# Row factors turned in 32x32 squares and stored in runs of 128 bytes, convolution states packed for their store, last columns stored later

## The chip, the cores and the metric

One Trainium2 chip, of which the kernel uses one core. The time is the device time of one execution in microseconds (us); the runs are compared by their median. The core has TensorE (PE in the profile, with its weight loads as PEld), VectorE (DVE), ScalarE (ACT), GpSimd (POOL) and SyncE (SP). SP computes nothing here: it issues transfers. ACT and POOL issue transfers as well. All transfers share 16 DMA engines. Each engine works through its own instructions in order, and waits on semaphores where an instruction needs another engine's result or a transfer.

## The reference

One layer of a hybrid decoder over 4096 prompt tokens and 64 sample tokens (8 sequences of 8), width 1024, all in float32:

```python
h = _rmsnorm(x, g_pre)
z = h @ w_in
cb, cc, ch, cg, q, k, v, ag, mq, mg = _split_cols(z)
u = cc * ch
up = jnp.concatenate([conv_buf, u], axis=1)
conv = conv_w[0] * up[:, 0:t] + conv_w[1] * up[:, 1:t + 1] + conv_w[2] * up[:, 2:t + 2]
out_a = jax.nn.silu(cg) * cb * conv
new_conv = up[:, -CONV_BUF:]
...
y = jnp.concatenate([out_a, out_b, out_c], axis=-1) @ w_out
return x + _rmsnorm(y, g_post), new_conv, new_k, new_v
```

`out_b` is sliding-window attention, `out_c` attention into 256 memory tokens. Two things matter here. `_rmsnorm` needs one factor per token, the reciprocal root of the mean square of its row. And `new_conv`, the last two columns of `u` of every sequence, is an output: `o_convs` for the 8 sample sequences, `o_convp` for the prompt.

## The kernel before

**Tiling.** The 4160 tokens (64 sample tokens first) form 8 blocks of 520, each of two halves of 260. Tokens lie along the free dimension and channels on the 128 partitions. The projection `w_in` is done in three phases, each over a part of its columns and over all 8 blocks. In phase 0 the first two blocks are plain products (`plain_block`, eight steps each); every other block of every phase takes seven products of a Strassen-like scheme, one step each, of block sums such as `T1`, `T2`. A step multiplies one half block, split into a high and a low part (`hi`, `lo`), by the weight parts, three passes in all. The third phase also prepares the memory keys and the first attention blocks; after it come attention and the output projection `w_out`.

**Row factors.** The factor of a token is the same number for all channels, so a block needs a row of 520 factors that is spread over the 128 partitions. `row_step` squares and sums 104 tokens at a time (tokens on partitions, `nat`), five times for a block, so the 520 sums stand in a tile `r` of 104 partitions by 5 columns: token 104 i + p of the block is at partition p, column i. POOL turns the sums into factors (lines 315 and 316). The factors of block 2 go another way (`rows_diag` and `rows_product`), and block 0's are used that way too in phase 0. For the seven blocks other than 2, POOL stores the 520 factors to a row in DRAM, `rowd`, each value 4 bytes from a place of its own (line 321). `rows_load` (line 284) then lets SP load that row to all partitions (`rb`), and `scale` (line 363) multiplies the block's half blocks by it. `row_queue` runs once in each step of phase 0; it sends the loads of `nat` and counts `row_spreads` down, so that `rows_load` is issued in the fourth step from the one that stored the row. It is in SP's order, so if the row has not been written, SP waits there with all loads behind it: the weights `ws` for later phases (line 234), the next `nat`, and the next half blocks `x` and `place` (line 271).

**Convolution states.** In phase 1 `finish_conv` (from line 475) makes `u`. In block 0 POOL multiplies the sample tokens' part into `us` (line 485), 128 x 8 x 10 values with two old columns first, and the last two columns of each sequence are stored from there: 1024 pieces of 8 bytes for each of two channel tiles. In the last block the two last columns (`ub_prev`, tile `tail`) are stored, 128 pieces of 8 bytes for each of the two tiles.

**Order.** In phase 0 and from phase 2 on, each engine keeps the order in which the program is written; in phase 1 the framework orders the work. `store` sends from POOL in phase 0. Later it puts the store on `late`, and `flush` issues it from SP in the next step. A transfer also waits until the transfer eight before it of the same kind (eight semaphores for those of POOL, eight for those of SP and ACT) has landed, since it takes over its semaphore.

Of the kernel before, what the change touches and what calls it, by code (L numbers as in the profile page):

```python
# [8 lines left out]
F32 = mybir.dt.float32  # L9
# [6 lines left out]
P = 128  # L16
# [5 lines left out]
NB = 8  # L22
# [30 lines left out]
def hybrid_layer(ctx: ExitStack, tc: tile.TileContext, a: dict):  # L53
# [22 lines left out]
    V, TE, S, G = (InOrder(engine) for engine in (nc.vector, nc.tensor, nc.scalar, nc.gpsimd))  # L76

    const = ctx.enter_context(tc.tile_pool(name="const", bufs=1))
    tiny = ctx.enter_context(tc.tile_pool(name="tiny", bufs=3))
# [9 lines left out]
    G.memset(mhalf, -0.5)  # L89
    gmem = const.tile([P, KT], F32, name="gmem")  # L90
    convw = const.tile([P, 2, 3], F32, name="convw")

    zs = const.tile([P, 14, NS], F32, name="zs")

# [3 lines left out]
    rowd = [tc.dram_tile([2 * HW], F32, name=f"rowd{b}") for b in range(NBLK)]  # L98
# [99 lines left out]
    def store(dst, src):  # L198
        if store_queue[0] is G:
            G.dma_start(dst, src)  # L200
        else:
            late.append(lambda: DMA.dma_start(dst, src))

    def temp(name):
        return tp.tile([P, 2 * HW if 1 in zp else 2 + 2 * HW], F32, tag="t", name=name)
# [69 lines left out]
    RG = 104  # L275
# [4 lines left out]
    row_loads, row_spreads = [], {}  # L280

    def rows_load(b, again=False):
        rows[b] = (temp(f"rb{b}")[:, : 2 * HW] if again else natp.tile([P, 2 * HW], F32, tag="rb", name=f"rb{b}"))
        DMA.dma_start(rows[b], rowd[b].partition_broadcast(P))

    def row_load(j):
        if j < 5 * NBLK:
            g = RG * j - NS
            if 2 <= j < 10 or 12 <= j < 14:
                t = (wa if j < 7 or j == 12 else wb).tile([P, 2, 512], F32, tag="w", name=f"nat{j}")  # L290
                t = nat[j] = t.rearrange("p a n -> p (a n)")
            else:
                t = nat[j] = natp.tile([P, D], F32, tag="nat", name=f"nat{j}")
            if g < 0:
                DMA.dma_start(t[:NS], a["x_s"])
                DMA.dma_start(t[NS:RG], a["x_p"][: RG - NS, :])
            else:
                DMA.dma_start(t[:RG], a["x_p"][g : g + RG, :])

    def row_step():  # L300

        j = sq[0]
        if j == 5 * NBLK:
            return
        b, i = divmod(j, 5)
        if i == 0:
            nat["r"] = tiny.tile([P, 8], F32, tag="r", name=f"r{b}", bufs=3)
        r, t = nat["r"], nat.pop(j)
        S.activation(t[:RG], t[:RG], AF.Square, accum_out=r[:RG, i : i + 1])  # L309
        if j in (10, 11) or j >= 14:  # L310
            row_loads.append(after_nat[0])
            after_nat[0] += 1
        sq[0] += 1
        if i == 4:
            G.tensor_scalar(r[:RG, 0:5], r[:RG, 0:5], 1.0 / D, EPS, op0=ALU.mult, op1=ALU.add)
            G.tensor_tensor(r[:RG, 0:5], r[:RG, 0:5], mhalf[:RG, 0:5], op=ALU.pow)
            if b in (0, PLAIN_BLOCKS):
                nat["factors"] = r
            if b == PLAIN_BLOCKS:
                return  # L320
            G.dma_start(rowd[b].rearrange("(i p) -> p i", p=RG), r[:RG, 0:5])
            if b > 0:
                row_spreads[b] = 4

    def rows_diag():

# [14 lines left out]
    def row_queue():  # L341

        for j in row_loads:
            row_load(j)
        row_loads.clear()
        for b in [b for b, n in row_spreads.items() if n == 1]:
            rows_load(b)
        for b in list(row_spreads):
            row_spreads[b] -= 1
            if row_spreads[b] == 0:  # L350
                del row_spreads[b]
# [68 lines left out]
    def flat(z):  # L420
        return z.rearrange("p a n -> p (a n)")
# [37 lines left out]
            V.tensor_copy(zs[:, zsi, :], th[:, :NS])  # L459
        store(md[idx, :, tokens(b)], th)  # L460

    ub_prev, us_of = [None, None], []

    def us_load():
        for ct in range(2):
# [9 lines left out]
    def finish_conv(b, ct, zc, zh, zg, zb):  # L475
        zc, zh, zg, zb = (flat(z) for z in (zc, zh, zg, zb))
        n = 2 * HW
        ns = NS if b == 0 else 0
        m = n - ns
        V.scalar_tensor_tensor(zg, zb, 0.5, zg, op0=ALU.mult, op1=ALU.mult)  # L480
        ub = temp(f"ub{b}_{ct}")[:, : 2 + m]
        if ns:
            us = us_of[ct]
            V.memset(ub[:, 0:2], 0.0)
            G.tensor_tensor(us[:, :, 2:10], zc[:, :ns].rearrange("p (b t) -> p b t", b=NB),
                            zh[:, :ns].rearrange("p (b t) -> p b t", b=NB), op=ALU.mult)
            store(a["o_convs"][ct], us[:, :, 8:10])
        else:
            V.tensor_copy(ub[:, 0:2], ub_prev[ct])
        V.tensor_tensor(ub[:, 2:], zc[:, ns:], zh[:, ns:], op=ALU.mult)  # L490
        ub_prev[ct] = tiny.tile([P, 2], F32, tag=f"tail{ct}", name=f"tail{b}_{ct}", bufs=2)
        V.tensor_copy(ub_prev[ct], ub[:, m : m + 2])
        if b == NBLK - 1:
            store(a["o_convp"][ct], ub_prev[ct])
        acc = temp(f"cacc{b}_{ct}")[:, :n]
        if ns:

            dst, t = (x[:, :ns].rearrange("p (b t) -> p b t", b=NB) for x in (acc, zc))
            G.tensor_scalar(dst, us[:, :, 0:8], convw[:, ct, 0:1], None, op0=ALU.mult)
            for i in (1, 2):  # L500
                G.tensor_scalar(t, us[:, :, i : i + 8], convw[:, ct, i : i + 1], None, op0=ALU.mult)
                G.tensor_tensor(dst, dst, t, op=ALU.add)
        for i in range(3):
            if i == 0:
                V.tensor_scalar(acc[:, ns:], ub[:, 0:m], convw[:, ct, 0:1], None, op0=ALU.mult)
            else:
                V.scalar_tensor_tensor(acc[:, ns:], ub[:, i : i + m], convw[:, ct, i : i + 1], acc[:, ns:], op0=ALU.mult, op1=ALU.add)
        V.tensor_tensor(acc[:, ns:], acc[:, ns:], zg[:, ns:], op=ALU.mult)
        if ns:
            G.tensor_tensor(mix_s[:, ct, :], acc[:, :ns], zg[:, :ns], op=ALU.mult)  # L510
        store(md[ct, :, 2 * HW * b + ns : 2 * HW * b + n], acc[:, ns:])
# [65 lines left out]
    def next_block(ph, b, p):  # L577

        nph, nb = (ph, b + 1) if b + 1 < NBLK else (ph + 1, 0)
        load = lambda o: lambda: x_of(nph, nb, o)  # L580
        ready = lambda o: lambda: x_ready(nph, nb, o)
        jobs = []
        if nph < 2:
            jobs += {0: "B11", 3: "B21 B12", 4: "B22"} .get(p, "").split() if ph == 0 else \
                    {0: "B11", 3: "B21", 4: "B12", 5: "B22"}.get(p, "").split()
            jobs = [load(o) for o in jobs]
        if ph == 0:
            jobs.insert(0, row_queue)
            if 1 <= p < 4:
                jobs.append(row_step)  # L590
        if p == (0 if nb else 1) and nph == 1 and nb < PLAIN_BLOCKS:
            jobs.append(lambda: rows_load(nb, nb > 0))
        if nph < 2:
            jobs += [ready(o) for o in {4: "B11", 5: "B21" if nph else "B21 B12", 6: "B12 B22" if nph else "B22"}.get(p, "").split()]
        if ph == 0 and 4 <= p < 6:
            jobs.append(row_step)
        if nph < 2:
            if p == 6:
                jobs.append(lambda: t_sum(nph, nb, "T1"))
        return jobs  # L600
# [286 lines left out]
    def v_load(k):  # L887
        third["v", k] = t = temp(f"vl{k}")[:, :512]
        DMA.dma_start(t, vd[:, NS + 512 * k : NS + 512 * k + 512])
# [91 lines left out]
    last = NBLK - 1  # L981
# [11 lines left out]
    def input_projection():  # L993
        for i, (ph, b, p) in enumerate(steps):
# [22 lines left out]
            jobs = list(pending.pop(i, ()))  # L1017
# [4 lines left out]
                jobs += next_block(ph, b, p)  # L1022
            if (ph, b, p) == (0, last, 2):
                jobs.append(us_load)
            if ph == 1 and NP_ * b + p + 2 in V_TURNS:
                jobs.append(lambda k=V_TURNS.index(NP_ * b + p + 2): v_load(k))
            if ph == 1 and NP_ * b + p in V_TURNS:
# [28 lines left out]
            if (ph, b, p) in SWITCH:  # L1056
                jobs = SWITCH[ph, b, p]() + jobs
# [660 lines left out]

    blocks = [Block(b) for b in (*range(31), 32, 31)]
    input_projection()  # L1720
    open_attention()
    chunk_load(2)
# [166 lines left out]
```

## Time and profile before

| | |
|---|---|
| median of 3 runs | 1458.19 us (1456.69 to 1459.25) |
| the profiled execution's own time | 1455.13 us |
| its span, first to last instruction | 1453.4 us |
| ACT busy | 756.0 us (52%) |
| POOL busy | 447.1 us (31%) |
| DMA | 337.27 MB, mean 232 GB/s |
| granted TensorE clock, mean | 0.999 |

The profile is of one execution. A row of the waits reads: engine and tile and line that waited, what it waited for, us in total, times, longest. A row of the windows reads: stretch in us from the span's start, its length, then busy us and instructions of PE, PEld, DVE, ACT and POOL, the granted clock, the DMA engines' busy share, and GB/s. A row of the timeline reads: start, length, engine, line, operation, out<-in, shapes, and in brackets the idle time ahead of it and what ended it. Program names carry no buffer numbers there: `lo_3T` is a low part in block 3, `place` a half block with a place of its own. SPq and POOLq are the queues' own instructions.

### The profile page before, as it was taken

What the parts mean: (1) busy time and instruction counts of PE and PEld (TensorE: products, weight loads), DVE (VectorE), ACT (ScalarE), POOL (GpSimd) and SP (SyncE); (2) the same over time, 40 slices, a digit from 0 to 9 for tenths busy, and PEclk for the clock granted to TensorE, in tenths of its full rate; (3) what the DMA queues carried; (4) which work ended last, traced back from release to release, by engine and by line L of the source; (5) the groups of instructions that cost most, each with busy time, mean ns of one, the idle gap of its engine ahead of it and who ended that gap; (6) DMA issues with size and microseconds to landing.
All of it is one profiled execution on the core that took longest, in us unless ns stands there. A gap on an engine that the chain in (4) does not pass through costs nothing.

```text
span 1453.4 us, 30932 instructions
## 1 busy us (share of the span) xinstructions
PE 1442.0 (99%) x11453; PEld 1324.3 (91%) x11453; DVE 1206.5 (83%) x1899; ACT 756.0 (52%) x1868; POOL 447.1 (31%) x622
## 2 busy tenths in 40 slices
PE   9999999999999999999999999999999999999998
PEld 9999999999999999999999999978777787777777
DVE  6879888899998877799678778998998889888853
ACT  6776665566522222234445534656566555655641
POOL 0223323212300000000002224275665566556661
PEclk9999999999999999999999999999999999999999
DMA  9999999896866644475987978999988899998773
GB/s 266 160 275 232 293 269 277 238 307 215 226 223 198 192 136 150 140 273 143 323 276 228 290 231 266 324 261 238 238 217 224 215 258 228 238 237 223 233 220 105
DMA packets 212124, 337.27 MB, mean 232 GB/s; under 512 B 55301, under 2 KB 126213, under 8 KB 211941
## 3 DMA queue, kind: packets, MB, share of 16 engines
q1 hardware_dynamic: 159189, 226.29, 52.7%
q0 software_dynamic: 44144, 78.68, 21.3%
q10 hardware_dynamic: 8640, 30.33, 6.7%
q8 instruction: 91, 1.49, 0.5%
q14 instruction: 60, 0.49, 0.1%
HBM read 192.48 MB, written 110.15 MB: 208 GB/s over the span
## 4 chain that ended last, share of the span: by engine, by line
PE 82%; DMA 8%; DVE 4%; issue 3%; ACT 2%; SPq 1%; POOL 1%; POOLq 0%; ACTq 0%; DVEq 0%
PE c L397 46%; PE y L1675 24%; PE pv L1144 5%; PE ws L1144 3%; DMA place<-in_xt 2%; PE xs L1144 2%; DMA nat<-in_x_p 2%; DMA wr_3A<-in_w_in 1%; PE mem_acc L825 1%; DMA md<-th 1%; DVE z L649 1%; DMA x_1B<-in_xt 1%; DMA vd<-v 1%; DMA wr_3S<-sd6S 1%; DMA w<-s 0%
## 5 line engine op out<-in xcount | busy, mean ns | idle before, releaser
L1675 PE MATMUL y<-wo,mh 128*128 128x512 f32 (+1 forms) x1040 | 328.7, 391 | 0.0
L403 DVE TENSOR_TENSOR z<-c,z 128x520 f32<-128x520 f32 (+1 forms) x308 | 193.6, 644 | 61.3 <-PE c L397 60.5
L1675 PEld LDWEIGHTS y<-wo,mh 128*128 128x128 f32 x1040 | 194.2, 188 | 52.4 <-DVE wmx L1303 5.4
L1675 PE MATMUL y<-wo,ml 128*128 128x512 f32 (+1 forms) x520 | 201.0, 387 | 0.0
L1347 POOL TENSOR_SCALAR s<-s,x 128x256 f32<-128x256 f32 x124 | 58.0, 480 | 199.1 <-DVE x L1342 193.5
L1675 PEld LDWEIGHTS y<-wo,ml 128*128 128x128 f32 x520 | 97.8, 188 | 18.5
L1313 ACT ACTIVATE s<-s,wnm 128x128 f32<-128x128 f32 x256 | 98.7, 387 | 0.0
L771 POOL MEMSET negs<- 128x1 f32 x1 | 0.1, 100 | 281.7 <-DVE w_2A L219 281.7
L1290 ACT COPY s<-ws 128x256 f32<-128x256 f32 x128 | 41.3, 378 | 77.4 <-PE ws L1144 68.5
L1705 POOL TENSOR_TENSOR xr<-yn,xr 128x1024 f32<-128x1024 f32 x29 | 69.3, 2390 | 18.4 <-ACT yn L1704 17.7
L1378 POOL TENSOR_SCALAR_AFFINE_SELECT wd<-w 128x512 f32<-128x512 f32 x64 | 60.2, 941 | 38.2 <-DMA w<-s 21.7
L1683 ACT ACTIVATE y<-y 128x512 f32<-128x512 f32 (+1 forms) x66 | 38.6, 585 | 52.8 <-DVE yn L1682 52.7
L1336 ACT ACTIVATE s<-xs,x 128x256 f32<-128x256 f32 x128 | 58.1, 461 | 0.0
L1682 DVE TENSOR_TENSOR yn<-y,gpost 128x512 f32<-128x512 f32 (+1 forms) x66 | 44.7, 677 | 16.0 <-PE y L1675 14.5
L1144 PEld LDWEIGHTS ws<-kst,q 64*128 64x128 f32 x768 | 47.7, 185 | 11.0 <-issue 9.5
L1378 POOL TENSOR_SCALAR_AFFINE_SELECT w<-w 128x512 f32<-128x512 f32 x64 | 55.5, 887 | 2.2
L1144 PE MATMUL ws<-kst,q 64*128 64x256 f32 x768 | 55.0, 288 | 0.0
L1294 DVE COPY_PREDICATED s<-wmask,ws 128x256 f32<-128x256 uint8 x124 | 48.0, 441 | 8.0 <-ACT s L1290 6.0
L309 ACT ACTIVATE nat<-nat 104x1024 f32<-104x1024 f32 x40 | 42.3, 1058 | 19.2 <-DMA nat<-in_x_p 19.2
L405 ACT COPY z<-c 128x520 f32<-128x520 f32 (+1 forms) x44 | 24.1, 553 | 53.0 <-PE c L397 50.0
L1313 ACT ACTIVATION_READ_ACCUMULATOR s<-s,wnm 128x1 f32 x256 | 47.9, 187 | 0.0
L200 POOL DMA_DIRECT2D md<-th x48 | 26.2, 547 | 66.9 <-DVE th L457 40.3
(970 smaller groups left out, 4805.6 us busy)
## 6 DMA issues: line engine op xcount, KB each, us to landing
w<-s SPq DMA_DIRECT2D x456, 64.0 KB
q<-qd POOLq DMA_DIRECT2D x32, 768.0 KB, 6.6
xr<-in_x_p SPq DMA_DIRECT2D x32, 512.0 KB
nat<-in_x_p SPq DMA_DIRECT2D x39, 416.0 KB
o_yp<-xr SPq DMA_DIRECT2D x31, 512.0 KB
md<-th POOLq DMA_DIRECT2D x48, 260.0 KB, 7.0
qd<-zh SPq DMA_DIRECT2D x48, 260.0 KB
qd<-z SPq DMA_DIRECT2D x48, 260.0 KB
```

The costliest lines, as they stand in the source:

```text
L309: S.activation(t[:RG], t[:RG], AF.Square, accum_out=r[:RG, i : i + 1])
L397: TE.matmul(bank[:, :HW], w[:, l, k * P : (k + 1) * P], h[r][:, k], start=first and i == 0, stop=last and i == 3 * KH - 1)
L403: add = lambda dst, other: V.tensor_tensor(dst, c, other, op=ALU.add)
L1144: ins = TE.matmul(o, w, x, **kw)
L1294: V.copy_predicated(to, squares(third["wmask"]), squares(s3[:, :, 0:P]))
L1313: S.activation(sm[:, h], sm[:, h], AF.Exp, bias=nm[:, h : h + 1], scale=SCALE, accum_out=den[:, h : h + 1])
L1336: S.activation(p[:, i], s[:, i].rearrange("p (a k j) -> p a k j", a=2, k=4), AF.Exp, bias=nm[:, i : i + 1], scale=SCALE, accum_out=den[:, ...
L1347: G.tensor_scalar(p[:, i], p[:, i], rd[:, i : i + 1], 0.5, op0=ALU.mult, op1=ALU.mult)
L1378: G.affine_select(out, src, pattern=[[32 * sign, 2], [0, 8], [sign, 32]], compare_op=op, fill=0.0, base=base * sign, channel_multiplier=-s ...
L1675: TE.matmul(acc, self.hl[l][:, k], wo[k][c0 // 512][:, r, c0 % 512 : c0 % 512 + c1 - c0], start=j == 0, stop=j == passes * KT - 1)
L1682: V.tensor_tensor(yn[:m, c0:c1], acc[:m], gpost[0][:m, c0:c1], op=ALU.mult)
L1705: total = G.tensor_tensor(self.xr, yn, self.xr, op=ALU.add)
```

## The change

Row factors: the factors are copied by POOL into the first 5 columns of a tile `turned` of 128 x 32. Two steps later in the count (n == 3) DVE transposes this tile in its 32x32 squares, so that each square holds 5 rows of 32 consecutive tokens, and POOL stores the four squares apart: three stores of 5 runs of 128 bytes and one of 5 runs of 32 bytes. The load of the row stays where it was (n == 1). Block 0 now takes the same way, without the early load.

Convolution states: POOL copies the two columns of `us` into a tile of 128 x 16 and that is stored, 64 bytes from each partition. The store of the prompt's last columns is put off to step (2, 3, 0), block 3 of phase 2.

```diff
+    turned = const.tile([P, 32], F32, name="turned")
+    G.memset(turned, 0.0)
...
-            G.dma_start(rowd[b].rearrange("(i p) -> p i", p=RG), r[:RG, 0:5])
-            if b > 0:
-                row_spreads[b] = 4
+            G.tensor_copy(turned[:RG, 0:5], r[:RG, 0:5])
+            row_spreads[b] = 4
...
-        for b in [b for b, n in row_spreads.items() if n == 1]:
+        for b in [b for b, n in row_spreads.items() if n == 3]:
+            V.transpose(turned, turned)
+            for g in range(0, RG, 32):
+                n = min(32, RG - g)
+                G.dma_start(rowd[b].rearrange("(i p) -> i p", p=RG)[:, g : g + n], turned[g : g + 5, :n])
+        for b in [b for b, n in row_spreads.items() if n == 1 and b > 0]:
             rows_load(b)
...
-            store(a["o_convs"][ct], us[:, :, 8:10])
+            last = tiny.tile([P, 16], F32, tag="x4", name=f"convs{ct}")
+            G.tensor_copy(last.rearrange("p (b t) -> p b t", b=NB), us[:, :, 8:10])
+            store(a["o_convs"][ct].rearrange("p b t -> p (b t)"), last)
...
-            store(a["o_convp"][ct], ub_prev[ct])
+            convp.append(lambda: store(a["o_convp"][ct], ub_prev[ct]))
...
+            if (ph, b, p) == (2, 3, 0):
+                jobs += convp
```

On PE, ACT and SP the instructions and their order are the same, but for what the two `o_convs` stores read and for the place of the two `o_convp` stores.

The first place is POOL's order in block 3 of phase 0, where the factors of block 4 go out; `md`, `qd`, `vd` and `hd_B` are stores of finished results. Before:

```order
L316 TENSOR_TENSOR r_1647<-r_1647,mhalf 104x5
L321 DMA rowd_82<-r_1647 104x5x1
L200 DMA md<-th_2_1948 128x520
L200 DMA md<-th_4_1965 128x520
L200 DMA hd_B_116<-place 128x1040
L200 DMA md<-th_6_2038 128x520
L200 DMA qd<-zh_0_2042 128x520
L200 DMA qd<-kl__2044 128x520
L200 DMA md<-th_3_2062 128x520
L200 DMA md<-th_5_2066 128x520
L200 DMA md<-th_7_2118 128x520
```

The same stretch of the changed kernel:

```order
L324 COPY turned<-r_1664 104x5
L203 DMA md<-th_2_1965 128x520
L203 DMA md<-th_4_1982 128x520
L203 DMA hd_B_118<-place 128x1040
L203 DMA md<-th_6_2055 128x520
L203 DMA qd<-zh_0_2059 128x520
L203 DMA qd<-kl__2061 128x520
L203 DMA md<-th_3_2079 128x520
L203 DMA md<-th_5_2083 128x520
L352 DMA rowd_84<-turned 5x32 x3
L352 DMA rowd_84<-turned 5x8
L203 DMA md<-th_7_2140 128x520
```

The store of the row has moved behind eight stores of results and has become four.

The second place is DVE's order in the same stretch; `lo_3T` are the low parts that TensorE reads next. Before:

```order
L457 SCALAR_TENSOR_TENSOR th_6_2038<-th_6_2038,z_2_2_0_1616 128x520
L439 TENSOR_TENSOR kl__2044<-z_2_2_0_1616,zh_0_2042 128x520
L457 SCALAR_TENSOR_TENSOR th_3_2062<-th_3_2062,z_2_0_1_1499 128x520
L457 SCALAR_TENSOR_TENSOR th_5_2066<-th_5_2066,z_2_0_1_1499 128x520
L386 TENSOR_TENSOR lo_3T_2087<-x_3T_2023,hi_3T_2086 128x1040
```

Now:

```order
L464 SCALAR_TENSOR_TENSOR th_6_2055<-th_6_2055,z_2_2_0_1628 128x520
L446 TENSOR_TENSOR kl__2061<-z_2_2_0_1628,zh_0_2059 128x520
L464 SCALAR_TENSOR_TENSOR th_3_2079<-th_3_2079,z_2_0_1_1511 128x520
L464 SCALAR_TENSOR_TENSOR th_5_2083<-th_5_2083,z_2_0_1_1511 128x520
L349 STREAM_TRANSPOSE turned<-turned 128x32
L393 TENSOR_TENSOR lo_3T_2109<-x_3T_2040,hi_3T_2108 128x1040
```

One transpose of 128 x 32 stands ahead of a low part.

The third place is POOL's order at the sample tokens' convolution in phase 1; `us` is the product with its two old columns. Before:

```order
L485 TENSOR_TENSOR us_4265<-z_0_0_0_4702,z_0_0_1_4628 128x8x8
L501 TENSOR_SCALAR z_0_0_0_4702<-us_4265,convw 128x64
L485 TENSOR_TENSOR us_4267<-z_0_2_0_4733,z_0_2_1_4663 128x8x8
L501 TENSOR_SCALAR z_0_2_0_4733<-us_4267,convw 128x64
L499 TENSOR_SCALAR cacc_0_5185<-us_4265,convw 128x64
```

Now:

```order
L492 TENSOR_TENSOR us_4302<-z_0_0_0_4739,z_0_0_1_4665 128x8x8
L495 COPY convs_5219<-us_4302 128x16
L510 TENSOR_SCALAR z_0_0_0_4739<-us_4302,convw 128x64
L492 TENSOR_TENSOR us_4304<-z_0_2_0_4770,z_0_2_1_4700 128x8x8
L495 COPY convs_5316<-us_4304 128x16
L510 TENSOR_SCALAR z_0_2_0_4770<-us_4304,convw 128x64
L508 TENSOR_SCALAR cacc_0_5224<-us_4302,convw 128x64
```

Each product is followed by a copy of its last columns, from which SP stores.

More of the change, by code (lines that the diff above doesn't have):

```diff
@@ L460, in finish_gate @@
         store(md[idx, :, tokens(b)], th)
-    ub_prev, us_of = [None, None], []
+    ub_prev, us_of, convp = [None, None], [], []
     def us_load():
```

## The prediction

> **What bounds the kernel now.** I read the page's busy times first, then the waits of TensorE, then the windows around those waits.
>
> ```profile
> span 1453.4 us, 30932 instructions
> PE 1442.0 (99%) x11453; PEld 1324.3 (91%) x11453; DVE 1206.5 (83%) x1899; ACT 756.0 (52%) x1868; POOL 447.1 (31%) x622
> ```
>
> ```profile
> PE idle L737 <- POOL mhalf L89: 1.5, 1, 1.5
> PE c L397 <- DVE lo_1T L386: 1.0, 1, 1.0
> PE c L397 <- DVE w_0A L739: 0.9, 1, 0.9
> PE c L397 <- DVE lo_1B L386: 0.7, 1, 0.7
> PE pv L1144 <- ACT y L1683: 0.3, 1, 0.3
> PE c L397 <- DVE lo_6B L386: 0.3, 1, 0.3
> PE c L397 <- DVE lo_2T L386: 0.2, 1, 0.2
> ```
>
> TensorE is busy 1442.0 of 1453.4 us. Of the 11.4 us left, these rows name 4.9; 2.4 of them (`mhalf`, `w_0A`) lie in the first 6 us, ahead of everything that the change touches. The rest lies in no wait that this view names. Within reach are four waits: 0.2 and 0.3 in phase 0 (block sums `lo_2T` and half block `lo_6B`), 0.7 and 1.0 at the convolution in phase 1 (`lo_1B`, `lo_1T`): 2.2 us in all. That is 0.15% of the span, while about 0.2% (2.9 us) is what a measurement of this kernel can tell from no change. A busy TensorE could hide slow matmuls, but it gets through the same number of them (36 in 4 us) in the slow transfer windows below as in the fast ones.
>
> **What the old stores cost the transfers.** The windows hold DVE's busy time in the third pair of columns, and DMA share and GB/s at the end.
>
> ```profile
> 140.00:144.00 4.00, 4.00 (x36) 4.00 (x35) 3.08 (x4) 1.07 (x1) 2.82 (x5) 1.00 1.20 234
> 144.00:148.00 4.00, 4.00 (x36) 4.00 (x35) 4.00 (x6) 3.78 (x7) 0.54 (x2) 1.00 0.58 37
> 148.00:152.00 4.00, 4.00 (x36) 4.00 (x35) 3.65 (x5) 0.89 (x2) 1.66 (x4) 1.00 1.02 214
> 152.00:156.00 4.00, 4.00 (x36) 4.00 (x36) 2.79 (x5) 3.81 (x7) 1.56 (x3) 1.00 1.08 385
> 294.00:298.00 4.00, 4.00 (x36) 4.00 (x36) 3.63 (x4) 2.79 (x5) 1.07 (x2) 1.00 1.02 402
> 431.00:435.00 4.00, 4.00 (x36) 4.00 (x35) 4.00 (x7) 0.00 (x0) 0.00 (x0) 1.00 0.94 301
> ```
>
> ```profile
> L321 POOL DMA_DIRECT2D rowd<-r x7: 990/1001/1177, 42.2 to 260.1; - x7
> DMA to landing us min/median/max: 8.7/11.5/14.5
> 140.47 1.00 POOL L321 DMA_DIRECT2D rowd<-r  x1 [0.30 <-POOL r L316]
> ```
>
> A row store goes out at 140.47, and in the 12 us from 140 the rate is 234, 37 and 214 GB/s against 385 behind it. The loss is (151 + 348 + 171) x 4 us = 2.7 MB, which is **7.0 us of transfer time** at 385 GB/s, for 520 values. At 294 the same `hd_B` stores run without a row store, at 402 GB/s, so it is the row store that slows them.
>
> The nearest row for the new stores is `vn`, in runs of 128 bytes, two of whose 32 stores go out at 431.14:
>
> ```profile
> L898 SPq DMA_DIRECT2D vn<-vq x32: 318/482/1467, 431.1 to 594.3; - x32
> ```
>
> Around them 301 GB/s are moved. So a run of 128 bytes does not stop the engines, and with 20 runs in place of 520 values I take the 7.0 us as gone, seven times. But TensorE's column reads 4.00 in all these windows. It waits for none of it: the cover is gone only where a load is the last thing to arrive.
>
> **The terms in phase 0.** That place is block 6, in the chain of work:
>
> ```profile
> 247.75 13.21 DMA place<-in_xt
> 266.51 1.55 PE c L397 x11
> ```
>
> The half block lands 13.21 us after its issue, at 260.96, and TensorE starts at 266.51, 0.3 late. With up to 7.0 us of transfers taken away at 220 to 231, it lands earlier, and that 0.3 goes. The 0.2 at `lo_2T` I count as gone too, though no row here ties it to a store. **Term: -0.5**, between -0.5 and 0. Next in line is DVE itself, 1 to 2 us behind.
>
> What is added: seven transposes, 28 stores in place of 7, seven small copies.
>
> ```profile
> L1359 DVE STREAM_TRANSPOSE s<-s 128x1024 f32<-128x1024 f32 x32 | 39.7, 1240 | 3.2 <-POOL s L1347 3.2
> L894 DVE STREAM_TRANSPOSE vq<-vl 128x512 f32<-128x512 f32 x8 | 5.6, 703 | 0.0
> L1559 POOL COPY sqb<-zs 64x64 f32<-64x64 f32 x8 | 2.0, 249 | 0.4
> 141.47 1.11 POOL L200 DMA_DIRECT2D md<-th  x2
> ```
>
> (1240 - 703) / 512 = 1.05 ns for a column, so 128 x 32 takes about 703 - 480 x 1.05 = 0.20 us, and seven take 1.4. They stand on DVE ahead of a low part that has slack (1.1 us at the least place, below), so they are covered: 0, and 1.4 if all showed. POOL issues a store in about 0.55, so four take 2.2 in place of 1.0; with a copy of 0.25 that is 1.5 us more for a block, on an engine that is busy 1.56 of 4 us there: 0. What waits behind it are the stores `md` and `vd`, which free tiles for ACT; at worst ACT is 1.5 us later, which is 0.4 past the least slack.
>
> **The load of the row.** It stays in place while its store moves behind eight others:
>
> ```profile
> 151.95 0.54 POOL L200 DMA_DIRECT2D md<-th  x1 [0.40 <-DVE place L376]
> 154.26 0.34 SPq L284 DMA_DIRECT2D rb<-rowd  x1
> 154.79 2.90 SPq L234 DMA_DIRECT2D ws0A<-in_w_in  x4
> md<-th POOLq DMA_DIRECT2D x48, 260.0 KB, 7.0
> w<-s POOLq DMA_DIRECT2D x56, 64.0 KB, 4.1
> ```
>
> The four stores start behind `md` at 152.5, and the last is issued at 154.1. It lands 7.0 us later if it queues like an `md`, and 4.1 if it is like the smallest transfers that POOL issues (`w`, 64 KB; a few KB may take less). So the load, due at 154.26, waits until 158 or 161: **SP stands 4 to 7 us, in blocks 3 to 7**, with four weight loads, a `nat` and the half blocks behind it. This is the new wait. I take 4, since the new stores are nearest to `w`, and hold it against the 7.0 us of transfers that are no longer ahead of those loads: they are issued later and land no later. Term 0; the upper end goes into the second rival.
>
> The Trainium skill, page "DMA: Bandwidth & Descriptors", speaks against this in "Rules for kernel authors" and "Anatomy of one DMA": coalesce small transfers, since each one from GpSimd has a fixed cost of about 2.0 us. By that rule four in series would take 8.0 us, the load would wait until 160.5, and with the slack of 1.1 us from the second rival below TensorE would wait 160.5 - 154.3 - 1.1 = 5.1: 1463.3. The trace does not put stores in series: the two `md` at 141.47 were issued in 1.11 us, though one takes 7.0 to land.
>
> **Convolution states.** Here TensorE waits most.
>
> ```profile
> 384.00:388.00 4.00, 3.29 (x29) 3.08 (x27) 4.00 (x5) 0.93 (x2) 3.53 (x3) 1.00 1.01 73
> 396.00:400.00 4.00, 3.00 (x26) 2.83 (x25) 4.00 (x9) 1.35 (x2) 1.56 (x3) 1.00 0.98 374
> L485 POOL TENSOR_TENSOR us<-z,z x2: 1246/1248/1251, 382.5 to 385.6; 128x64 f32<-128x64 f32 x2
> 385.40 1.23 DVE L376 TENSOR_TENSOR x_1T<-place,x_1B 128x1040 f32<-128x1040 f32 x1
> 386.55 1.36 DVE L386 TENSOR_TENSOR lo_1B<-x_1B,hi_1B 128x1040 fp32r<-128x1040 f32 x1
> ```
>
> The rate falls to 73 GB/s with the 8-byte stores, but DVE is busy 4.00 of 4.00: TensorE waits for DVE's own work, not for a load, so faster stores give nothing. POOL gets two copies, 0.25 each by the row above and up to 1.25 beside DVE, as `us`. DVE's operations of this size take 1.36 at times beside POOL, against 1.23, so two more might be 0.13 longer. **Term: +0.2**, between 0 and +0.5, and -1.7 if I am wrong about DVE (first rival).
>
> The last columns: SP stood for their tile and held little.
>
> ```profile
> SPq L202 <- DVE tail L492: 16.2, 2, 13.5
> 664.00:668.00 4.00, 4.00 (x36) 4.00 (x35) 4.00 (x10) 2.04 (x3) 0.00 (x0) 1.00 0.60 28
> ```
>
> TensorE reads 4.00 here too. At their new place the 256 pieces might slow transfers for 4 us, as in this window; no wait of TensorE is named in phase 2. Term 0, between 0 and +1.
>
> **Sum.** -0.5 + 0 + 0.2 + 0 = -0.3. Against the profiled execution, 1455.13 us (span 1453.4 and 1.7 around it), that is 1454.8. The median of the runs, 1458.19, lies 3.06 above it, so the forecast is 1458.19 - 0.3 = **1457.9 us**.
>
> **The rivals.**
> 1. *The phase 1 waits go too*, because faster stores let DVE's inputs come sooner. -0.5 - 1.7 = -2.2, so 1456.0. Against it: DVE has no idle time in those windows. Chance 0.08.
> 2. *SP's new wait reaches TensorE* (slower). The place is block 6, where ACT waits for `nat` and the high and low parts follow at once:
>
> ```profile
> 256.81 1.06 ACT L309 ACTIVATE nat<-nat 104x1024 f32<-104x1024 f32 x1 [0.67 <-DMA nat<-in_x_p]
> 258.94 1.25 DVE L386 TENSOR_TENSOR lo_6B<-x_6B,hi_6B 128x1040 fp32r<-128x1040 f32 x1 [0.92 <-ACT hi_6B L385]
> 261.32 0.64 PE L397 MATMUL c<-lo_6B,w_0A 128*128 128x260 f32 x4
> ```
>
> The low part ends at 260.19 and is read at 261.32: slack 1.1 us. If SP stands for 7.0 and the loads land later by as much, TensorE waits 5.9 there: 1458.2 + 5.9 = 1464.1. It decides from the point where the delay exceeds what the transfers gain by more than 1.1. Against it: the gain is itself 7.0. Chance 0.09.
> 3. *The change does not do what it says*: short runs stall the engines all the same, or the four stores together as much as one. Then nothing of the 0.5 comes and 0.2 stays: 1458.4. Against it: `vn`. Chance 0.07.
>
> **How the numbers follow.** The forecast has the other 0.76. Its own range is that of three runs, 1.3 either way: 1456.5 to 1459.3. The range given reaches to the first rival with half its scatter and partly towards the second: 1455.4 to 1460.6. Faster by over 0.2% needs more than all four waits: 0.06, for scatter around the first rival. Slower by over 0.2% is the second rival: 0.09. Within: 0.85.
>
> **What would show it.** Right: no window under 200 GB/s behind a row store; `lo_6B` and `lo_2T` gone from TensorE's waits, `lo_1B` and `lo_1T` still there; SP's wait ahead of line 287 (the row's load) some us long in blocks 3 to 7, and its loads landing by the same time. Wrong: TensorE waits in blocks 3 to 7 for a low part behind an `x`, `place` or `nat`; or windows as slow as before, with 20 runs in them.

## The result, and the profile after

| | median | range | runs |
|---|---|---|---|
| kernel before | 1457.44 us | 1455.25 to 1459.25 | 6 |
| changed kernel | 1465.42 us | 1463.79 to 1468.19 | 6 |

The changed kernel is **slower by 8.0 us**: ratio 1.0058, 95% interval 1.0047 to 1.0069. The execution profiled took 1465.31 us. First the page of the changed kernel, with its span and busy times, and the waits of TensorE:

```profile
span 1463.6 us, 30973 instructions
PE 1447.7 (99%) x11453; PEld 1330.0 (91%) x11453; DVE 1210.7 (83%) x1906; ACT 758.2 (52%) x1868; POOL 460.9 (31%) x653
```

```profile
PE ws L1155 <- DMA q<-qd: 4.8, 1, 4.8
PE idle L746 <- POOL mhalf L89: 1.5, 1, 1.5
PE pv L1155 <- ACT y L1694: 0.9, 4, 0.3
PE c L404 <- DVE w_0A L748: 0.9, 1, 0.9
PE c L404 <- DVE lo_1T L393: 0.7, 1, 0.7
```

Two things are new. TensorE waits 4.8 us for `q<-qd`, a load of attention queries, far behind every line that the diff touches. And TensorE, with the same 11,453 matmuls, is busy 5.7 us longer.

**What was predicted for phase 0 did come.** The stores of row factors (line view of L352), SP's wait for the row, and the windows around four stores at 151 to 153 us:

```profile
L352 POOL DMA_DIRECT2D rowd<-turned x28: 521/527/751, 48.9 to 272.7; - x28
DMA to landing us min/median/max: 3.0/5.0/7.5
```

```profile
SPq L287 <- DMA rowd<-turned: 33.4, 5, 9.2
```

```profile
148.00:152.00 4.00, 4.00 (x36) 4.00 (x35) 4.00 (x7) 3.53 (x6) 3.67 (x7) 1.00 0.87 293
152.00:156.00 4.00, 4.00 (x35) 4.00 (x35) 3.46 (x6) 2.12 (x3) 2.19 (x5) 1.00 0.88 248
156.00:160.00 4.00, 4.00 (x36) 4.00 (x35) 2.39 (x3) 0.62 (x1) 0.00 (x0) 1.00 0.38 121
```

A store lands in 5.0 us where it took 11.5, and 248 GB/s flow beside it where it was 37. The 121 GB/s behind it are no stall of the transfers: they are busy 0.38 of the time, because SP stands at the row's load and asks for none. TensorE's column stays at 4.00.

**Where the time went.** Matched matmul by matmul, the changed kernel is 2.0 us behind the kernel before when the latter is at 960 us, and 8.8 us behind at 980. The timeline of that place, the two rows of POOL and then one of SP's queue, in the kernel before and in the changed one:

```profile
964.33 0.57 POOL L1696 TENSOR_TENSOR yst<-yst,mhalf 128x1 f32<-128x1 f32 x1
964.87 0.89 POOL L1182 DMA_DIRECT2D q<-qd  x1
965.79 0.45 SPq L1190 DMA_DIRECT2D place<-md  x1
```

```profile
966.32 0.58 POOL L1707 TENSOR_TENSOR yst<-yst,mhalf 128x1 f32<-128x1 f32 x1
968.19 0.90 POOL L1193 DMA_DIRECT2D q<-qd  x1 [1.28 <-issue]
967.76 0.44 SPq L1201 DMA_DIRECT2D place<-md  x1
```

From its issue to its landing that one query load took, before and after (view of its line):

```profile
DMA to landing us min/median/max: 5.9/5.9/5.9
```

```profile
DMA to landing us min/median/max: 11.6/11.6/11.6
```

In the kernel before, the second half of a query load goes out 0.92 us ahead of SP's `place<-md` (1 MB), and lands in 5.9 us. In the changed one POOL stands 1.28 us with nothing to wait for ("issue"), the load goes out 0.43 us behind the 1 MB, and takes 11.6 us. The windows of the changed kernel show what follows (the third number from the end is the granted clock):

```profile
967.00:972.00 5.00, 5.00 (x23) 4.13 (x22) 4.86 (x11) 3.82 (x18) 3.08 (x6) 1.00 0.84 238
972.00:977.00 5.00, 2.97 (x14) 2.06 (x12) 3.33 (x4) 0.79 (x1) 4.05 (x5) 1.00 1.07 333
977.00:982.00 5.00, 2.20 (x20) 2.20 (x22) 0.32 (x1) 0.73 (x3) 0.00 (x0) 0.51 1.30 281
982.00:987.00 5.00, 5.00 (x53) 3.77 (x52) 4.64 (x7) 2.32 (x5) 3.74 (x3) 0.81 0.60 134
```

TensorE is idle for 2.0 us in the second row and 2.8 in the third, and from 977.1 to 983.9 its clock is halved. The load landed at 979.75, so 4.2 us of work ran at half speed, which costs 2.1: 4.8 + 2.1 = 6.9, the whole step. The Trainium skill, page "TensorE: Matmul & The Clock Gate", Part 1, says that an idle window of about 3.4 us halves the clock, until a busy window follows. The trace agrees in part: the 6.827 us at 0.5 are two such windows, but the clock fell 2.1 us after TensorE's last matmul had ended (at 974.97), so less than a whole window without work was enough here.

**The rest** is not a wait. From 420 to 640 us, in phase 1, TensorE has no idle time in either kernel, and yet it starts fewer matmuls (the first row is the kernel before, the second the changed one):

```profile
420.00:640.00 220.00, 220.00 (x1862) 220.00 (x1861) 185.82 (x263) 55.81 (x65) 0.00 (x0) 1.00 0.53 170
```

```profile
420.00:640.00 220.00, 220.00 (x1853) 220.00 (x1852) 185.03 (x262) 54.43 (x63) 0.00 (x0) 1.00 0.53 167
```

By their starts in the trace, the same 1,859 matmuls take 219.98 us before and 221.02 us after, 0.47% more, at clock 1.00. Behind 980 us this pair of executions drifts apart by another 1.5 us up to 1400 us. No wait of over 0.3 us goes with that, and the medians differ by 8.0 us where this pair differs by 10.2, so I give it no cause.

### The profile page after: what moved, and what is told of

Read it like the earlier page. It is cut to its first block, busy times and chain, and to the rows that moved or that the text cites. A ratio compares the mean times of both kernels' runs of the same rounds, so it can differ in the third digit from the quotient of the medians.

```text
span 1463.6 us, 30973 instructions
## 1 busy us (share of the span) xinstructions
PE 1447.7 (99%) x11453; PEld 1330.0 (91%) x11453; DVE 1210.7 (83%) x1906; ACT 758.2 (52%) x1868; POOL 460.9 (31%) x653
## 3 DMA queue, kind: packets, MB, share of 16 engines
q8 instruction: 91, 1.49, 0.5%
## 4 chain that ended last, share of the span: by engine, by line
PE 86%; DVE 4%; issue 4%; DMA 3%; POOL 1%; SPq 1%; ACT 1%; DVEq 0%; POOLq 0%; ACTq 0%
PE c L404 55%; PE y L1686 21%; PE pv L1155 5%; PE ws L1155 3%; PE xs L1155 1%; DMA q<-qd 1%; SPq L1373 1%; PE mem_acc L834 1%; DMA mix<-md 1%; DMA wr_3S<-sd6S 1%; DMA vd<-v 0%; DMA w<-s 0%; ACT s L1324 0%; DVE yn L1693 0%; DMA o_yp<-xr 0%
## 5 line engine op out<-in xcount | busy, mean ns | idle before, releaser
L1715 ACT ACTIVATE yn<-yn,yst 128x1024 f32<-128x1024 f32 x29 | 33.4, 1152 | 21.5 <-POOL yst L1707 21.5
L1340 DVE TENSOR_REDUCE x<-xs 128x2 f32<-128x512 f32 x64 | 43.7, 684 | 0.0
```

The costliest lines, as they stand in the source:

```text
L1340: V.tensor_reduce(mx, s, axis=AX.X, op=ALU.max)
```

## The experiments

Two questions: why does POOL stand still at the query load, and what slows the matmuls? The theories have names in the expectations. For the first, **ring**, **instructions** (called **position** in the first four), **shift** and the prediction's second rival, **row load**. For the second, **addresses** and **transfers**. Each median stands beside runs of the kernel before on the same chip.

**Split the change.** The row factors alone, then the other two edits alone.

```diff
-            last = tiny.tile([P, 16], F32, tag="x4", name=f"convs{ct}")
...
+            store(a["o_convs"][ct], us[:, :, 8:10])
...
-            convp.append(lambda: store(a["o_convp"][ct], ub_prev[ct]))
+            store(a["o_convp"][ct], ub_prev[ct])
```

> The kernel before with the row factors' part of the change alone (the turn and the four stores of each block); the convolution states and the last columns as before. GpSimd runs 31 more instructions (7 copies more, 21 more stores, a memset, and a few waits) ahead of the attention. Theory 'position' (GpSimd stands still for some 1.3 us after a given number of its own instructions, and in the changed kernel this falls on the second half of a query load, which then queues behind SyncE's 2 MB): a wait of TensorE for q<-qd of some 4 to 5 us near 970 us and a stretch of TensorE clock 0.5 behind it, time 1463 to 1466; with a count near but not equal, no such wait and 1455 to 1458. Theory 'row load' (the prediction's second rival: SyncE held for 5 to 9 us at each block's row load costs TensorE time in phases 0 and 1): no q<-qd wait needed, 1460 to 1465, the loss before 360 us. Theory 'tails' (the loss comes of the convolution states or the late last columns): 1455 to 1458.

Measured: 1466.01 us beside 1456.23, ratio 1.0064 (1.0048 to 1.0080). TensorE waits 5.9 us for `q<-qd`, and POOL stands still ahead of it (timeline):

```profile
969.69 0.90 POOL L1189 DMA_DIRECT2D q<-qd  x1 [1.70 <-issue]
```

> The kernel before with the packed convolution states and the late store of the last columns alone; row factors as before. Theory 'position': GpSimd has only two more instructions than before, so the query load is where it was: no q<-qd wait, 1456.5 to 1458.5. Theory 'row load': the same, 1456.5 to 1458.5. Theory 'tails': the whole loss, 1463 to 1466, with the q<-qd wait if the later o_convp store moves SyncE's queue.

Measured: 1456.38 us, ratio 0.9998 (0.9988 to 1.0008), no such wait. In this kernel the stand still is elsewhere, as it was in the kernel before (929.11, 3.82 us):

```profile
930.12 0.90 POOL L1194 DMA_DIRECT2D mix<-md  x1 [3.83 <-issue]
```

So the row factors hold the whole loss, and both kernels have one stand still, which falls on different transfers. ("issue" alone does not prove one: in e2_tails the view also puts 3.52 us ahead of an `md` store at 186.91 down to it, where the kernel before, at 187.23, waits 3.53 us for VectorE's `th`.)

**Is it a number of instructions?** The kernel before, with POOL's count raised and its transfers untouched:

```diff
+    spare = const.tile([P, 1], F32, name="spare")
...
+            if (ph, b, p) == (2, 2, 0):
+                jobs.append(lambda: [G.memset(spare, 0.0) for _ in range(33)])
```

> The kernel before with 33 do-nothing GpSimd memsets (128x1, one tile that nothing reads) in phase 2, where GpSimd has nothing else to do: as many more instructions as the change gives GpSimd, and not one transfer more. Theory 'position': the q<-qd wait of 4 to 5 us and the 0.5 clock behind it, 1462 to 1465, though no row factor, store or load is touched. Theories 'row load', 'tails' and 'shift' (phase 3 starts some 2 us later, and that alone changes who comes first): no such wait, 1456 to 1458.5.

Measured: 1460.54 us, ratio 1.0025 (1.0016 to 1.0035), no `q<-qd` wait; POOL stands at the same load as before, for the same time:

```profile
933.20 0.90 POOL L1193 DMA_DIRECT2D mix<-md  x1 [3.83 <-issue]
```

"Position" falls: 33 instructions more move nothing. The 4 us were expected by no theory. The same 1,859 matmuls took 221.54 us, in phase 1, before any of the memsets; the only other thing that this kernel has is a tile of 4 bytes. That is the second question.

**Is the late load the loss?** The changed kernel with the half query load issued behind the first half:

```diff
-            if self.b == 5:
-                chunks[3].load_queries(1)
...
-                for fn in query_loads(3)[:2]:
+                for fn in query_loads(3):
```

> The changed kernel, and the second half of chunk 3's query load issued directly behind the first half, some 16 us earlier than now and ahead of SyncE's 2 MB. If that load's late issue is the cause of the loss, by whatever theory: no q<-qd wait, TensorE's clock 1.0 all through, 1456 to 1459. Theory 'row load': the loss stays, 1462 to 1466.

Measured: 1460.02 us, ratio 1.0020 (1.0010 to 1.0029): no such wait, no halved clock there, and 1.0 us above the range. POOL now stands at the fourth of eight `w` stores:

```profile
966.18 2.53 POOL L1371 DMA_DIRECT2D w<-s  x5 [1.99 <-issue]
```

So the place is not tied to a transfer either: with that load's descriptors put ahead of the `w` stores, one of these is hit. Counting descriptors (an estimate: runs divided over 16 engines, and one end mark for each transfer), POOL's sum at the stand still lies in 1,885 to 1,950 in the kernel before, 1,882 to 1,931 in the changed one, and 1,916 to 1,919 here. One number fits all three. The next four test it, and the tile's place.

```diff
-    turned = const.tile([P, 32], F32, name="turned")
-    G.memset(turned, 0.0)
...
+            if ph == 0:
+                turned = own.enter_context(tc.tile_pool(name="turned", bufs=1)).tile([P, 32], F32, name="turned")
+                G.memset(turned, 0.0)
```

> The changed kernel, and the 128 bytes of the tile turned lie behind all other tiles of phase 0, where nothing is moved by them, instead of among the constants, where they move every tile that is allocated later by 128 bytes. Theory 'addresses' (in the changed kernel, in e1_rows and in e4_q_early TensorE takes 0.47% longer over the same matmuls of phases 0 and 1, 221.0 us for 220.0, which starts with the first block and has no wait to go with it; the tile's 128 bytes are its cause): 220.0 us for the 1,859 matmuls from 420 us on, and some 1.9 us less in all than the changed kernel, with the q<-qd wait still there: 1463 to 1464.5. Rival 'transfers' (the new stores or loads slow TensorE's reads in these phases): 221.0 us as in the changed kernel, 1464.5 to 1466.5.

Measured: 1463.30 us beside 1455.29, ratio 1.0048 (1.0034 to 1.0062), `q<-qd` wait 5.3 us, and the matmuls back at 219.98 us:

```profile
420.00:640.00 220.00, 220.00 (x1862) 220.00 (x1861) 185.81 (x262) 56.97 (x67) 0.00 (x0) 1.00 0.54 172
```

The stores and loads are the changed kernel's, only the addresses are not: "addresses" stands, "transfers" falls.

```diff
+            if (ph, b, p) == (1, 3, 0):
+                jobs.append(lambda: [G.dma_start(turned[:128, : 4 * 1].rearrange("p (j n) -> p j n", j=1),
+                                                 vn[512 * 1 : 512 * 1 + 128, :].rearrange("p (j n) -> p j n", n=128)[:, :, :4]) for _ in range(16)])
...
```

> The changed kernel, and in phase 1, where GpSimd has nothing to do, 24 loads on GpSimd's queue into turned, which nothing reads by then: 16 of 128 runs of 16 bytes and 8 of 64 runs. They add as many descriptors to each of the 16 engines, 184, as the change takes away (a row store of 520 4-byte pieces was 33 and one end mark, its four new ones are 8 in all, times 7). Theory 'ring' (GpSimd stands still for 1 to 4 us when the count of descriptors that it has written reaches some 1,917 for an engine, which in the kernel before falls on the mix load at 929 us, where nothing is late, and in the changed one on the half query load at 968 us): the stand still is back at the mix load, no q<-qd wait, clock 1.0 all through, 1457 to 1460. Rival 'instructions' (it comes after a number of GpSimd's instructions): with 24 more instructions it falls elsewhere too, but not at the mix load. Rivals 'row load' and 'shift': the loss stays, 1464 to 1466.5.

Measured: 1458.14 us, ratio 1.0015 (1.0006 to 1.0024), no `q<-qd` wait. With the descriptors put back, so is the stand still:

```profile
933.22 0.90 POOL L1207 DMA_DIRECT2D mix<-md  x1 [3.94 <-issue]
```

> The kernel before, its row factors untouched, with a 128-byte tile among the constants and 24 loads on GpSimd's queue into it in phase 1 (12 of 1,024 runs of 16 bytes, 12 of 16 runs), 804 descriptors more for an engine, so that the count at the half query load at 965 us goes from 2,064 to 2,868, which is that at which GpSimd stood still a second time in the changed kernel (1,241 us, 0.62 us). Theory 'ring': GpSimd stands still at that query load, it comes behind SyncE's 2 MB, the q<-qd wait of 4 to 6 us and the 0.5 clock are there, though the row stores are those of before: with 1.9 us for the tile's place 1463 to 1466. Rivals 'row load', 'instructions' and 'shift': no such wait, 1457 to 1460.

Measured: 1459.53 us, ratio 1.0028 (1.0018 to 1.0038), and **no** `q<-qd` wait: the expectation of "ring" missed, and the time lies in the range of its rivals. There is no second stand still at 2,868, so the 0.62 us at 1,241 us was something else (0.5 to 0.7 us stand ahead of that same query load in seven kernels, whatever their count). But the first one left the `mix` load and stands at the tenth added load, which spans 1,885 to 1,950 in this kernel:

```profile
481.43 0.88 POOL L1030 DMA_DIRECT2D spare<-vn  x1 [3.76 <-DMA spare<-vn]
489.15 0.88 POOL L1030 DMA_DIRECT2D spare<-vn  x1 [6.83 <-issue]
495.12 0.89 POOL L1030 DMA_DIRECT2D spare<-vn  x1 [5.10 <-DMA spare<-vn]
```

Each of these loads follows when its predecessor lands, some 0.3 us later; the middle one comes 1.5 us after its predecessor landed (487.69 by the semaphore). So the stand still goes with the count, 440 us earlier and with nothing of the attention near it. The 128-byte tile among the constants again gave 221.02 us for the matmuls.

> The changed kernel with turned behind the other tiles of its phase, as in e5_place_of_tile, and the 24 loads of e6_more_descriptors. Theories 'ring' and 'addresses' together: neither the q<-qd wait nor the 0.47%, and TensorE's waits for lo_2T, lo_6B and lo_1B stay away: 1454.5 to 1457.5, no slower than the kernel before. If something else of the change costs time (rival 'row load'): 1459 or more.

Its edits are those of e5_place_of_tile and e6_more_descriptors, but that the tile is allocated once more behind the others in phase 1, where the loads write into it. Measured: 1455.47 us, ratio 1.0000 (0.9991 to 1.0009): both mended, the loss is gone, and the change gains nothing either. Of the waits that were to stay away, `lo_1B` is there with 0.2 us.

**A small dose**, against the rival that any load in phase 1 mends it:

```diff
+            if (ph, b, p) == (1, 3, 0):
+                jobs.append(lambda: [G.dma_start(turned[:16, :4], vn[512:528, :4]) for _ in range(8)])
```

> The changed kernel with 8 loads of 16 runs of 16 bytes on GpSimd's queue in phase 1, 16 descriptors more for an engine instead of the 184 of e6_more_descriptors; the half query load then covers the count from 1,898 to 1,947, and 1,917 is still in it. Theory 'ring': the loss stays, q<-qd wait 4 to 6 us, 1463.5 to 1466.5. Rival 'any load in phase 1 moves it' (e6_more_descriptors mended it by its loads' presence, their time or their instructions): no such wait, 1457 to 1460.

Measured: 1465.84 us beside 1456.77, ratio 1.0065 (1.0050 to 1.0080), `q<-qd` wait 5.6 us, stand still of 1.49 us at that load. The rival falls.

**The loss without the change.** One line of the kernel before:

```diff
-            G.dma_start(rowd[b].rearrange("(i p) -> p i", p=RG), r[:RG, 0:5])
+            G.dma_start(rowd[b].rearrange("(p i) -> p i", p=RG), r[:RG, 0:5])
```

> The kernel before with one edit: the row store writes its 104 x 5 factors in the order in which they lie, 104 runs of 20 bytes, instead of 520 pieces of 4 bytes (so the row loads read them in another order, and the output's row factors are wrong ones; amounts and instructions are the same). One store for each block as before, no tile, no turn, no instruction more. A store is then 7 descriptors and an end mark for an engine instead of 33 and one, 182 less in seven, and the half query load at 965 us covers the count from 1,882 to 1,931, as in the changed kernel. Theory 'ring': GpSimd stands still there for 1.2 to 1.7 us, the q<-qd wait of 4 to 6 us and 6.8 us of clock 0.5 are there, nothing else of the change is: 1460.5 to 1464, and 219.98 us for the matmuls from 420 us on. Rivals 'row load', 'instructions' and 'shift': as before or up to 1 us faster by the shorter store, 1454 to 1457.

Measured: 1458.79 us beside 1456.77, ratio 1.0014 (1.0004 to 1.0024), no `q<-qd` wait: a second miss of "ring" as I had sized it, and the time lies above its rivals' range too. POOL stands neither at `mix` nor at that half load, but at the next query load, which in other traces follows `yst` by 0.5 us:

```profile
976.86 0.56 POOL L1696 TENSOR_TENSOR yst<-yst,mhalf 128x1 f32<-128x1 f32 x1 [0.64 <-DVE yst L1695]
979.25 0.92 POOL L1182 DMA_DIRECT2D q<-qd  x1 [1.83 <-PE pv L1144]
```

(The view names TensorE as the releaser there, so that this is the stand still is read only from the 0.5 us in the other traces.) I took it that such a store counts for 2 descriptors and an end mark, and that fewer blocks should do what seven overdid. The packets in the trace speak against that price: 98 of them on GpSimd's queue, 14 for each store, hold 140 bytes, which is seven runs of 20.

```diff
+            G.dma_start(rowd[b].rearrange("(p i) -> p i" if b < 5 else "(i p) -> p i", p=RG), r[:RG, 0:5])
```

> The kernel before with the edit of e9_runs_of_20 in the first five blocks only; the last two store in pieces of 4 bytes as before (five blocks' row factors reach the output in another order). In e9_runs_of_20 GpSimd's stand still was not at the half query load but at the next query load, at 979.25 us (the load followed its neighbour by 0.53 us in the other runs, there by 2.39 us), where TensorE waits for nothing: by that a store of 20-byte runs is not the 7 descriptors I took, but 2 at the most and an end mark. With 3 in all, five blocks take 155 away, the half query load then covers the count from 1,909 to 1,958 and 1,917 is in it. Theory 'ring': the stand still of 1.2 to 2 us at that load, the q<-qd wait of 4 to 6 us, 6.8 us of clock 0.5, 1460.5 to 1464.5, with no tile, no turn and not one instruction more than before. Every rival: 1455 to 1459, as e9_runs_of_20.

The edit does less than the expectation says: `b < 5` takes in blocks 0, 1, 3 and 4 alone, since block 2 has no such store, so four stores change and three stay. With the 3 descriptors assumed, the half query load would then cover 1,940 to 1,989, and 1,917 would not be in it. Measured: 1463.98 us beside 1455.27, ratio 1.0061 (1.0045 to 1.0077): the forecast wait came, but by luck of the sizing. POOL stands at the last `w` store, directly ahead of the half query load, which so comes behind SP's `place<-md` at 967.30; TensorE waits 4.0 us, and its clock is halved for 6.827:

```profile
967.53 0.50 POOL L1362 DMA_DIRECT2D w<-s  x1 [1.94 <-issue]
968.05 0.58 POOL L1696 TENSOR_TENSOR yst<-yst,mhalf 128x1 f32<-128x1 f32 x1
968.60 0.89 POOL L1182 DMA_DIRECT2D q<-qd  x1
```

No tile, no turn, no instruction more, and the matmuls at 219.98 us: the order of the bytes in four early stores makes a later load late. The number itself is not settled. At 8 for a store of 20-byte runs, the sum at the stand still is 1,948 to 1,997 in e9_runs_of_20 and 1,957 to 1,960 here, both above the 1,917 of the others, here by 40. With other prices one number does lie in all thirteen stand stills: 1,980, for instance, at 41 for a store of 520 pieces, 8 for one of 104 runs and 17 for the four new stores together. But these prices are fitted, and many sets of them fit.

**A version without added loads:** e5_place_of_tile, and the row stores on SP's queue.

```diff
-                G.dma_start(rowd[b].rearrange("(i p) -> i p", p=RG)[:, g : g + n], turned[g : g + 5, :n])
+                DMA.dma_start(rowd[b].rearrange("(i p) -> i p", p=RG)[:, g : g + n], turned[g : g + 5, :n])
```

> The changed kernel with turned behind the other tiles of phase 0 and the four row stores of a block on SyncE's queue instead of GpSimd's; nothing else is added. GpSimd's count is 56 lower, and 1,917 falls on the first half of the next chunk's query load, the harmless place of e9_runs_of_20. Theories 'ring' and 'addresses': no q<-qd wait, 219.98 us for the matmuls from 420 us on, 1454.5 to 1457.5. Rival 'row load': SyncE now waits for the turn and issues 28 stores more, which delays the loads behind them in phase 0: new waits of TensorE before 340 us, 1459 to 1463.

Measured: 1456.25 us beside 1455.27, ratio 1.0003 (0.9993 to 1.0013), no `q<-qd` wait. SP waits more than ever in phase 0:

```profile
SPq L354 <- DVE turned L351: 77.7, 7, 19.8
```

and TensorE, matched with the kernel before, is level with it at 340 us (0.8 us ahead in that pair of executions). "Row load" falls. The stand still wasn't seen at the load that I had named for this kernel; where it fell is open. None of these versions is measurably faster than the kernel before.

## Why the prediction was wrong

- **The four waits within reach (term -0.5).** `lo_6B` and `lo_2T` are gone, as forecast. But they are gone in e2_tails, e3_pad33 and e7_descriptors_before too, which have the old row stores, and e2_tails has a new `lo_5B` of 0.7 us instead. Such waits come and go with the row stores untouched; the term took scatter for an effect.
- **The old stores' 7.0 us of transfers, hidden.** Right: the slow windows went, and TensorE gained nothing from it, which e8_both_mended puts at 1.0000 (0.9991 to 1.0009).
- **What is added: "0".** This is the step that failed, twice. It priced the seven copies, transposes and 28 stores by their time on POOL and DVE in phase 0, and in phase 0 that was right. It did not ask what else they leave behind. The stores take POOL's count of descriptors down, by some 180 for an engine in my estimate, which moves POOL's stand still from a load with slack to one with little, some 700 us behind the last row store: 7.8 us between e5_place_of_tile and e8_both_mended, and 1458.14 in e6_more_descriptors, where the count was put back. And the tile's 128 bytes move the addresses behind it: 2.7 us between e6_more_descriptors and e8_both_mended.
- **SP's new wait (term 0).** Right in kind and hidden, but sized low: 33.4 us in five waits are 6.7 each, the longest 9.2, where 4 was taken and 7 was the upper end. The second rival, 1464.1, came near the time by another mechanism; e12_stores_on_SyncE, with SP held for 77.7 us, lost nothing.
- **The rule that was weighed (1463.3)**, of the Trainium skill's page "DMA: Bandwidth & Descriptors", came near the time too, and not for its reason. The four stores of a block were issued 0.52 us apart, and the last landed 0.6 to 3.7 us behind the first, not 6 us (three times 2.0). The load that was to wait until 160.5 went out at 158.74, and TensorE waited for nothing there.
- **Convolution states and last columns (+0.2, 0).** Right within 0.9988 to 1.0008. The first rival's waits: `lo_1B` is gone here and back at 0.7 in e5_place_of_tile, again scatter.
- **Behind phase 2 no term was set.** The evidence was in the trace of before: POOL's 3.82 us of "issue" ahead of the `mix` load, and a query load that landed at 970.81 for a first use at 972.6, so 1.8 us of slack beside 2 MB of SP's transfers.

Open: what in POOL stands still. The trace has no record of it. No load of instructions (queues 8 and 14 of the transfers) starts in the 6 us ahead of it in the kernels before and after. VectorE does not hold it either: beside the half query load it runs the same work in both kernels, and in the changed one POOL goes on at 968.19, in the middle of VectorE's `xr` (967.28 to 968.56). The Trainium skill, page "DMA: Bandwidth & Descriptors", section "SWDGE vs HWDGE vs iDMA", says that GpSimd writes pairs of descriptors into rings that the engines drain. A ring that fills or wraps would behave so, but no run here shows the ring itself, and the count of 1,917 is an estimate: it fits the kernels before and after and nine experiments, is too low for e9_runs_of_20 and e11_five_blocks, by 40 for the latter, and no stand still was seen in e12_stores_on_SyncE.

## What to carry to other kernels

A changed transfer on GpSimd's queue can cost time hundreds of microseconds later: look through the trace of before for places where GpSimd stands on "issue", and ask which load would be late if one of them moved. When a new tile is added, put it behind the others, and compare TensorE's number of matmuls in a window where it never idles. The five waits of TensorE of 4.0 to 5.9 us here each cost 1.8 to 3.0 us more, by the halved clock behind them.

## What the runs showed of the hardware that was not expected

- In thirteen of the fourteen kernels GpSimd stands still once, for 1.3 to 2.4 us (3.8 to 3.9 at `mix`, where it waits 1.5 for TensorE in any case: 928.68 in the changed kernel), at a place that moves with the number and shape of the transfers it issued before (e4, e6, e7, e9, e11) and not with its number of instructions (e3). In e12 none was seen.
- Operand addresses change TensorE's speed at clock 1.00: 219.98 us for 1,859 matmuls with the tiles where they were (before, e2, e5, e8, e9, e11, e12), 221.02 with 128 bytes ahead of them (after, e1, e4, e6, e7, e10), 221.54 with a 4-byte tile (e3). Between the first two groups, some three of every 48 matmuls, 6 to 10 ns longer each, make 0.9 of the 1.04 us. What in the addresses does it was not tried.
- 520 values stored 4 bytes at a time held the transfers at 37 GB/s, and yet storing them in longer runs gained nothing that could be measured (e8, e12).
